# Half of the weight tiles loaded as fp32 on a hardware queue and cast on ScalarE, in a DMA-bound matmul of four windows

One core of one Trainium2 chip. The metric is the device time of one execution in microseconds (us).

## The reference

```python
B, S, D, W = 4, 4096, 4096, 64          # x: [B,S,D] fp32, w: [D,D] fp32
for b in range(B):
    o = int(offsets[b])
    results.append(x[b, o:o+W] @ w)     # [64,4096] @ [4096,4096]
return np.stack(results)                # [4,64,4096] fp32
```

The whole of w (67.1 MB) has to be read once, with 4.2 MB of x, and 4.2 MB are written. Each weight is used for only 256 rows, so the loads decide the time.

## The kernel before

Every tile of w, 128 rows (one k) by 2048 columns (one half `ng` of the output), is loaded by a DMA issued from GpSimd that casts fp32 to fp16 on its way. Only the first 128 rows of w (k = 0, both halves; called row 0 below) come as fp32 on ScalarE's queue and are cast there. The windows of x come as four casting DMAs, each to 64 partitions. They are transposed on TensorE, and then the matmuls follow the tiles of w as they land.

```python
    wh_pool = ctx.enter_context(tc.tile_pool(name="wh", bufs=24))
    ...
    nc.scalar.dma_start(out=w0_32[:], in_=w[0:P, :])
    def load(ng, ki):
        t = wh_pool.tile([P, NG], fp16, name="wh", tag="wh")
        nc.gpsimd.dma_start(out=t[:], in_=w[ki*P:(ki+1)*P, ng*NG:(ng+1)*NG])
        return t[:]
    wh[(0, 1)] = load(0, 1)
    ...                                  # for each b: o = offset of the window
        nc.gpsimd.dma_start(out=x16[g][m*WIN:(m+1)*WIN, :], in_=x[b][bass.ds(o, WIN), :])
    ...                                  # all other tiles in order of use; the
    ...                                  # very last one as four [128,512] pieces
    for ng in range(n_ng):               # 2 halves
        for ki in range(n_k - 1 if last else n_k):
            for g in range(G):           # 2 pairs of windows
                for j in range(n_sub):   # 4 PSUM banks each
                    mm(g, j, ki, wh[(ng, ki)][:, j*NT:(j+1)*NT], ki == 0, ki == n_k - 1)
        ...                              # first half: evict to stage[g]
    for g in range(G):                   # issued after all loads of w
        nc.gpsimd.dma_start(out=out[2*g:2*g+2, :, 0:NG], in_=stage[g][:])
    for j in range(n_sub):               # last k of the second half
        for g in range(G):
            mm(g, j, ki, wlast[j][:], False, True)
            ...                          # evict on ScalarE (g 0) or VectorE (g 1)
            q[g].dma_start(out=out[2*g:2*g+2, :, cs:cs+NT], in_=s[:])   # 256 KB each
```

The 2 MB of the first half's stores stand behind all loads in the casting queue. They keep the DMA engines busy while the last matmuls and evictions run.

## Time and profile before

| | before |
|---|---|
| time | 184.98 us median (184.97 to 185.01, 3 runs) |
| span of the profiled run | 183.1 us |
| last matmul of w ends, last packet of a DMA | 172.5 us, 181.3 us |

From the page of the kernel before: the bytes moved in 40 slices of the span, the chain of work that ended last, the largest group of instructions, and the issues of w tiles (size as written, median time to landing).

```profile
GB/s 179 348 221 215 207 213 215 215 214 211 213 211 214 215 213 214 214 216 214 211 214 212 213 213 214 213 215 214 215 213 212 213 214 212 213 213 205 387 403 172
...
DMA wh<-in_w_dram 90%; ACT sth L150 1%; PE bank L117 1%; ACTq L153 1%; POOLq L60 0%; POOLq L168 0%
...
L117 PE MATMUL bank<-wh,xT 128*128 128x512 f16 x488 | 113.8, 378 | 28.6 <-DMA wh<-in_w_dram 28.6
...
wh<-in_w_dram POOLq DMA_DIRECT2D x61, 512.0 KB, 19.1
```

Loads of w make up 90% of the chain, and TensorE waits for them. The slices count bytes as written. A casting load reads twice what it writes, so 213 GB/s there is 426 GB/s of reading, and the stores at the end (387 and 403 GB/s) are not a faster stage. All rates below are therefore given on the source side: casting bytes count twice, plain ones once.

The view of the DMA queues of before, for 15 to 29 us (the end of x, then w) and for 60 to 150 us; columns are packets, MB written, share of 16 engines' time. A packet is one row of a transfer; packets of 4 bytes, about one in nine, are counted with them:

```profile
q0 software_dynamic: 693, 2.97, 104.6%
```

The timeline of before (start, duration, engine, line, operation) when x arrives, and at its end:

```profile
16.17 3.57 PE L103 MATMUL bank<-identity,xrow 128*128 128x128 f16 x32 [16.17 <-DMA xrow<-in_x_dram]
...
24.35 2.07 PE L117 MATMUL bank<-w0half,xT 128*128 128x512 f16 x8
```

```profile
168.93 1.89 PE L117 MATMUL bank<-wh,xT 128*128 128x512 f16 x8 [0.57 <-DMA wh<-in_w_dram]
...
170.65 1.89 PE L117 MATMUL bank<-wl,xT 128*128 128x512 f16 x8
171.07 0.58 ACT L150 COPY sth<-bank 128x512 f32<-128x512 f32 x1 [73.36 <-PE bank L117]
...
171.69 0.34 ACTq L153 DMA_DIRECT2D out_dram<-sth  x1
```

The first matmul of w starts at 24.35 us. A tile needs 1.89 us of matmul and TensorE waits another 0.57 us for the next, so TensorE is never far behind the loads. The first store of the last group leaves 0.6 us after the first eviction (the copy of a finished sum out of PSUM) starts.

### The profile page before, as it was taken

Reading aid. Unit: us, or ns where it says so; the run is one execution under the profiler, and the core shown is the slowest. Engines: PE = TensorE matmul, PEld = TensorE weight load, DVE = VectorE, ACT = ScalarE, POOL = GpSimd, SP = SyncE. Lnnn points to the kernel's source line nnn. Section 1 sums busy time; section 2 is a strip of 40 time slices with the busy share of each in tenths; the row PEclk is TensorE's granted clock in tenths of the full one; section 3 lists DMA queues with packets and bytes.
Section 4 is the critical chain, followed back from the end, with each engine's and each line's share of the span. In section 5 each row is a group of like instructions: output and inputs, shape, how many; then the busy total and the mean of one; then the engine's idle time right before and its main releaser. Section 6 shows DMA issues by size and latency. Waiting matters only on the chain.

```text
span 183.1 us, 1380 instructions
## 1 busy us (share of the span) xinstructions
PE 126.3 (69%) x576; PEld 56.4 (31%) x576; DVE 10.5 (6%) x16; ACT 14.1 (8%) x19; POOL 38.3 (21%) x77
## 2 busy tenths in 40 slices
PE   0004799988877777887779878777777877777600
PEld 0004664433333233333324333323232333333200
DVE  0002530000000000000005000000000000000500
ACT  2081430000000000000013000000000000000310
POOL 4612221222222112222221222222122222210000
PEclk9999999999999999999999999999999999999965
DMA  6999999999999999999999999999999999999994
GB/s 179 348 221 215 207 213 215 215 214 211 213 211 214 215 213 214 214 216 214 211 214 212 213 213 214 213 215 214 215 213 212 213 214 212 213 213 205 387 403 172
DMA packets 11271, 40.97 MB, mean 224 GB/s; under 512 B 1282, under 2 KB 1794, under 8 KB 10626
## 3 DMA queue, kind: packets, MB, share of 16 engines
q0 software_dynamic: 9968, 36.70, 97.0%
q10 hardware_dynamic: 720, 3.15, 4.7%
q1 hardware_dynamic: 578, 1.05, 1.5%
q8 instruction: 4, 0.07, 0.1%
q14 instruction: 1, 0.01, 0.0%
HBM read 71.30 MB, written 4.19 MB: 412 GB/s over the span
## 4 chain that ended last, share of the span: by engine, by line
DMA 90%; issue 2%; ACT 1%; PE 1%; ACTq 1%; POOLq 0%
DMA wh<-in_w_dram 90%; ACT sth L150 1%; PE bank L117 1%; ACTq L153 1%; POOLq L60 0%; POOLq L168 0%
## 5 line engine op out<-in xcount | busy, mean ns | idle before, releaser
L117 PE MATMUL bank<-wh,xT 128*128 128x512 f16 x488 | 113.8, 378 | 28.6 <-DMA wh<-in_w_dram 28.6
L117 PEld LDWEIGHTS <-xT 128*128 128x128 f16 x512 | 49.8, 97 | 98.0 <-issue 44.1
L60 POOL DMA_DIRECT2D wh<-in_w_dram x61 | 32.4, 531 | 112.5 <-DMA wh<-in_w_dram 100.2
L103 PE MATMUL bank<-identity,xrow 128*128 128x128 f16 x64 | 7.1, 311 | 17.4 <-DMA xrow<-in_x_dram 17.4
L103 PEld LDWEIGHTS <-xrow 128*128 128x128 f16 x64 | 6.7, 147 | 17.6 <-issue 17.6
L150 ACT COPY sth<-bank 128x512 f32<-128x512 f32 x4 | 2.3, 586 | 74.6 <-PE bank L117 73.8
L137 ACT COPY stage<-bank 128x512 f32<-128x512 f32 x4 | 2.1, 600 | 70.5 <-PE bank L117 70.5
L112 DVE CAST xT<-bank 128x512 f16<-128x512 f32 x8 | 5.5, 691 | 19.3 <-PE bank L103 19.3
L152 DVE COPY sth<-bank 128x512 f32<-128x512 f32 x4 | 2.5, 683 | 72.3 <-PE bank L117 72.3
L139 DVE COPY stage<-bank 128x512 f32<-128x512 f32 x4 | 2.5, 682 | 71.7 <-PE bank L117 71.7
L114 ACT CAST xT<-bank 128x512 f16<-128x512 f32 x8 | 4.7, 586 | 6.9 <-PE bank L103 6.9
L117 PE MATMUL bank<-w0half,xT 128*128 128x512 f16 x16 | 4.3, 390 | 0.2 <-DVE stage L139 0.2
L90 POOL DMA_DIRECT2D wl<-in_w_dram x4 | 2.1, 527 | 7.5 <-DMA wh<-in_w_dram 7.5
L77 POOL DMA_DIRECT2D xrow<-in_x_dram x4 | 2.1, 520 | 2.2 <-issue 2.2
L97 ACT CAST w0half<-w0row 128x2048 f16<-128x2048 f32 x1 | 1.9, 1897 | 7.4 <-DMA w0row<-in_w_dram 7.4
L141 POOL DMA_DIRECT2D out_dram<-stage x2 | 1.1, 534 | 4.2 <-DMA wh<-in_w_dram 4.2
L98 ACT CAST w0half<-w0row 128x2048 f16<-128x2048 f32 x1 | 1.9, 1893 | 0.0
L117 PE MATMUL bank<-wl,xT 128*128 128x512 f16 x8 | 1.9, 379 | 0.0
L97 ACT ACT_TABLE_LOAD x1 | 1.3, 1283 | 1.3 <-PEq L168 1.3
masks.py:199 POOL TENSOR_SCALAR_AFFINE_SELECT identity<-identity 128x128 f16<-128x128 f16 x1 | 0.3, 287 | 0.1
masks.py:197 POOL MEMSET identity<- 128x128 f16 x1 | 0.2, 223 | 0.0
L168 POOL MEMSET const-float32-0.0<- 128x1 f32 x1 | 0.1, 98 | 0.4 <-issue 0.4
(3 smaller groups left out, 0.3 us busy)
## 6 DMA issues: line engine op xcount, KB each, us to landing
wh<-in_w_dram POOLq DMA_DIRECT2D x61, 512.0 KB, 19.1
w0row<-in_w_dram ACTq DMA_DIRECT2D x1, 2048.0 KB, 9.0
xrow<-in_x_dram POOLq DMA_DIRECT2D x4, 512.0 KB, 12.3
out_dram<-stage POOLq DMA_DIRECT2D x2, 1024.0 KB, 12.1
out_dram<-sth ACTq DMA_DIRECT2D x4, 256.0 KB, 6.5
out_dram<-sth SPq DMA_DIRECT2D x4, 256.0 KB, 6.6
wl<-in_w_dram POOLq DMA_DIRECT2D x4, 128.0 KB, 14.9
off_t<-in_offsets_dram SPq DMA_DIRECT2D x1, 0.0 KB
```

The source lines that it names most:

```text
L60: nc.gpsimd.dma_start(out=t[:], in_=w[ki * P : (ki + 1) * P, ng * NG : (ng + 1) * NG])
L77: nc.gpsimd.dma_start(out=x16[g][m * WIN : (m + 1) * WIN, :], in_=x[b][bass.ds(o, WIN), :])
L90: nc.gpsimd.dma_start(out=t[:], in_=w[ki * P : (ki + 1) * P, cs : cs + NT])
L97: nc.scalar.copy(out=w0_16[:, :NG], in_=w0_32[:, :NG])
L103: nc.tensor.matmul(out=ps[t][:, i * P : (i + 1) * P], lhsT=x16[g][:, k * P : (k + 1) * P], rhs=identity[:], start=True, stop=True,)
L112: nc.vector.tensor_copy(out=dst, in_=ps[t][:])
L114: nc.scalar.copy(out=dst, in_=ps[t][:])
L117: nc.tensor.matmul(out=ps[4 * g + j][:], lhsT=xT[g][:, ki * P : (ki + 1) * P], rhs=rhs, start=start, stop=stop,)
L137: nc.scalar.copy(out=dst, in_=ps[4 * g + j][:])
L139: nc.vector.tensor_copy(out=dst, in_=ps[4 * g + j][:])
L150: nc.scalar.copy(out=s[:], in_=ps[4 * g + j][:])
L152: nc.vector.tensor_copy(out=s[:], in_=ps[4 * g + j][:])
```

## The change

The intent is to use both ways of loading at once: even k tiles of w come as fp32 on SP's hardware queue and ScalarE, 8% busy before, casts them; odd ones stay casting loads. The last four tiles are all casting loads. The last tile is loaded whole, and the last group goes out as two 1 MB stores instead of eight of 256 KB.

```diff
-    wh_pool = ctx.enter_context(tc.tile_pool(name="wh", bufs=24))
+    wg_pool = ctx.enter_context(tc.tile_pool(name="wg", bufs=4))
+    wf_pool = ctx.enter_context(tc.tile_pool(name="wf", bufs=5))
+    wh_pool = ctx.enter_context(tc.tile_pool(name="wh", bufs=12))
 ...
     def load(ng, ki):
+        src = w[ki * P : (ki + 1) * P, ng * NG : (ng + 1) * NG]
+        if ki % 2 == 0 and (ng, ki) < (n_ng - 1, n_k - 4):
+            t = wf_pool.tile([P, NG], fp32, name="wf", tag="wf")
+            nc.sync.dma_start(out=t[:], in_=src)
+            wf[(ng, ki)] = t
+            return None
         t = wh_pool.tile([P, NG], fp16, name="wh", tag="wh")
 ...
-        for ki in range(n_k - 1 if last else n_k):
+        for ki in range(n_k):
+            if (ng, ki) in wf:
+                t = wg_pool.tile([P, NG], fp16, name="wg", tag="wg")
+                nc.scalar.copy(out=t[:], in_=wf[(ng, ki)][:])
+                wh[(ng, ki)] = t[:]
 ...                               # (the four pieces of the last tile are gone)
+            (q[g] if last else nc.gpsimd).dma_start(
+                out=out[2 * g : 2 * g + 2, :, ng * NG : (ng + 1) * NG],
+                in_=stage[ng][g][:],
+            )
```

## The prediction

> **What bounds it.** The DMA engines. The chain of waits is 90% loads of w; the slice table has DMA at 9 in 38 of 40 slices, tensor clock 9 throughout the stream. The issue table shows 61 w tiles landing in 19.1 us each with eight in flight; the chain shows eight per 19.66 us, 2.46 us a tile, so 1.05 MB read at 427 GB/s. The GB/s row says 213 because it counts the fp16 bytes written. A tile needs only 1.89 us of matmul (timeline), so TensorE waits 0.55 us per tile on the load (28.6 us in all).
>
> **Is a plain fp32 load cheaper?** Hardly. Packet records: the fp32 row 0 of w alone passed a 16 KB packet per engine every 611 ns, 429 GB/s read; casting packets pass 8 KB each 307 ns, 427 GB/s. The cast writes half the bytes but reads the same, and the time follows the bytes read. The Trainium skill, "DMA: Bandwidth & Descriptors", section "Issuing engines are not separate DMA queues", says all queues run on the same 16 engines; the trace agrees: while both queues were busy (5.5 to 8.5 us) an engine alternated one fp32 16 KB packet and one casting 8 KB packet every 923 ns, together 427 GB/s. So "both at once" adds no bandwidth: 71.3 MB read and 4.2 MB written remain, about 178 us of packets.
>
> **Removed:** 28 casting loads and their issue (0.53 us each) on GpSimd, off the chain. The last tile no longer goes in four pieces of 1 KB rows (3.1 against 2.46 us), and the last stores no longer use 2 KB rows (84 ns a packet against 309 for 8 KB): about 0.7 and 0.45 us gained.
>
> **Added:** 28 casts on ScalarE, 1.9 us each (the casts of row 0), 53 us; ScalarE was 8% busy; off the chain unless they come late. The last group's stores wait for all four evictions per half: the first leaves about 2.6 us after the first bank is done, against 0.6. ScalarE evictions no longer wait on issues (2.4 us instead of 3.7).
>
> **Moved.** Five fp32 tiles now compete with x at the start: the second half of x, landing at 20.6 us, should land near 27 to 30, first w matmul 24.4 to about 33. TensorE has slack to catch up. Afterwards odd and even tiles share the engines packet by packet, 4.9 us each; evens lead, so evens finish near 150 us, then about eight casting tiles remain, at 2.46 us. Each odd then frees two tiles (3.8 us of matmul): TensorE should lag the last landing (about 170 us) by 3 to 5 us instead of 1.4. The 2 MB of first-half stores cover 4.9 us; the engines should then stand idle 1 to 4 us before the final 2 MB (4.9 us). Worked forward with these durations, an estimate: span 183.5 to 186.5, time 1.9 more than the span as before.
>
> **Prediction:** 186.5 us, range 182.5 to 192. Chances: faster by over 2% 0.04, within 2% 0.70, slower by over 2% 0.26.
>
> **Shows it right:** read rate in the stream (bytes written weighted for the cast) still 425 to 430 GB/s; ScalarE busy near 64 us; first w matmul near 33 us; fp32 queue done near 150 us, the casting queue last; a dip of DMA between the first-half and last stores.
>
> **Makes it wrong:** the split of the engines. If the casting queue gets over about 57% the evens land last, and behind the last lie a cast and six tiles of matmul (13 us): 190 to 200. If mixing slows packets by a few per cent: 189. If mixing hides bubbles between packets and the tail stays covered: 182.

## More of the kernel before

```profile
q0 software_dynamic: 5252, 19.15, 106.0%
```

From 60 to 150 us that is 2 x 19.15 MB in 90 us, 425.6 GB/s read. This is close to what the Trainium skill's "HBM Reference" (section "Specifications (TRN2)") gives for a core that streams alone, about 425 GB/s, bounded by its 16 DMA engines.

## The result

| | before | changed |
|---|---|---|
| time, median (range, runs) | 185.0 us (184.97 to 185.09, 4) | 187.55 us (186.73 to 187.89, 4) |
| ratio, 95% interval | | 1.0131 (1.0097 to 1.0164) |
| span of the profiled run | 183.1 us | 186.0 us |
| first matmul of w | 24.35 us | 33.55 us |
| last packet of a casting load of w | 171.2 us | 174.7 us |
| last packet of a DMA | 181.3 us | 184.7 us |

A ratio here is the mean time of one kernel's fast runs over the mean of the other's of the same rounds, so it is not quite the ratio of the medians. The change made the kernel 1.3% slower, which is inside 2%. Part of the 3.4 us between the last packets comes back after them: the span ends 1.8 us after the last packet before and 1.3 us after it in the changed kernel.

The page of the changed kernel:

```profile
GB/s 183 383 306 268 263 268 290 312 286 313 321 310 321 313 320 315 319 318 314 314 314 316 315 319 311 321 313 320 314 318 315 319 320 225 213 212 214 369 308 282
...
DMA 79%; PE 12%; issue 3%; DVE 1%; POOLq 1%; POOL 1%; DVEq 0%
...
L111 PE MATMUL bank<-wh,xT 128*128 128x512 f16 x272 | 63.5, 378 | 29.3 <-DMA wh<-in_w_dram 29.3
...
L129 ACT CAST wg<-wf 128x2048 f16<-128x2048 f32 x28 | 52.5, 1903 | 56.9 <-DMA wf<-in_w_dram 53.9
...
wf<-in_w_dram SPq DMA_DIRECT2D x28, 1024.0 KB, 22.8
wh<-in_w_dram POOLq DMA_DIRECT2D x34, 512.0 KB, 39.1
```

The row of GB/s looks half as fast again as before, 316 against 213, and that is the trap of this profile: fp32 bytes written are not cast bytes written. ScalarE's 28 casts take 52.5 us and the engine waits for data in between, so they are no bottleneck. The mean of 1,903 ns agrees with an estimate from the Trainium skill, "ScalarE: Activation LUTs", section "What ACT_TABLE_LOAD costs", which gives 186 ns + 0.833 ns per element for an ACTIVATE with immediate scale and bias: 1,892 ns for 2,048 elements, if a cast counts as one.

The view of the DMA queues of the changed kernel, 15 to 29 us (x beside fp32 tiles):

```profile
q0 software_dynamic: 260, 1.72, 58.9%
q1 hardware_dynamic: 271, 1.96, 43.7%
```

And 60 to 150 us:

```profile
q1 hardware_dynamic: 2598, 18.94, 51.9%
q0 software_dynamic: 2597, 9.46, 51.8%
```

In the stream the read rate is (2 x 9.46 + 18.94) / 90 = 420.7 GB/s against 425.6, and at 15 to 29 us it is (2 x 1.72 + 1.96) / 14 = 386 GB/s. The two queues got 2,597 and 2,598 packets: an even split. This agrees with the Trainium skill, "DMA: Bandwidth & Descriptors", section "Queues, rings and completion order", which says that an engine takes the queues that have work in turn, a packet at a time. The counts show the equal turns, not how many rows an engine takes in one turn. Both shares together are 103.7% of the engines' time against 106.0% (packets overlap a little, hence over 100). A packet itself took no longer, 322 ns in the median against 324; the next one began later.

The smaller number of buffers is a rival: 12 for casting loads and 5 for fp32 ones, instead of 24. The page speaks against it. At 4.9 us a tile on each queue, landing times of 22.8 and 39.1 us mean that more than four fp32 tiles and about eight casting ones were under way at a time. And the loss is even: by the packet records the rate was 412 to 422 GB/s in every 5 us from 30 to 155 us, against 421 to 427 in before.

The timeline of the changed kernel when x arrives and at its end:

```profile
22.39 3.57 PE L97 MATMUL bank<-identity,xrow 128*128 128x128 f16 x32 [22.39 <-DMA xrow<-in_x_dram]
...
33.55 2.36 PE L111 MATMUL bank<-w0half,xT 128*128 128x512 f16 x8
```

```profile
155.80 1.90 ACT L129 CAST wg<-wf 128x2048 f16<-128x2048 f32 x1 [3.03 <-DMA wf<-in_w_dram]
...
169.24 8.80 PE L111 MATMUL bank<-wh,xT 128*128 128x512 f16 x40
176.56 2.05 ACT L138 COPY stage<-bank 128x512 f32<-128x512 f32 x4 [18.86 <-PE bank L111]
...
178.65 0.36 ACTq L142 DMA_DIRECT2D out_dram<-stage  x1
```

The last fp32 tile is cast at 155.8 us and only casting loads are left. The last store waits for its evictions and leaves at 178.65 us. The engine table of the changed kernel, in stretches of 2 us, shows the gap that this leaves (after the length come the busy times of PE, PEld, DVE, ACT and POOL, then the clock; the last two columns are DMA share and GB/s written):

```profile
178.00:180.00 2.00, 0.04 (x1) 0.00 (x0) 1.91 (x4) 0.62 (x2) 0.00 (x0) 1.00 0.47 197
180.00:182.00 2.00, 0.00 (x0) 0.00 (x0) 0.00 (x0) 0.00 (x0) 0.00 (x0) 0.82 0.96 393
```

**Where the time went.** Every kernel here moves the same 75.5 MB, counted at the source. So the time lost in a stretch can be worked out from the trace's packet records: its length minus its bytes divided by 427 GB/s, the rate of casting loads in before. The sums close: the last packet comes 3.4 us later, and the rows differ by 3.3 us. The last columns are experiments told below.

| DMA time lost, us | before | changed | a: casting only | c: x first | c2: x first, fewer fp32 | e: x in 128 rows |
|---|---|---|---|---|---|---|
| 0 to 10 us | 2.92 | 2.96 | 2.98 | 2.98 | 3.05 | 2.88 |
| 10 to 30 (x) | -0.02 | 1.48 | -0.03 | 0.03 | 0.02 | 0.15 |
| 30 to 155 (stream) | 0.21 | 1.78 | 0.21 | 1.79 | 1.67 | 1.84 |
| 155 to 170 | 0.14 | 0.01 | 0.01 | 0.13 | 0.01 | 0.01 |
| 170 to the last packet | 1.07 | 1.43 | 1.17 | 2.68 | 1.02 | 1.52 |
| of these, in the last 1 us | 0.75 | 0.09 | 0.85 | 0.09 | 0.79 | 0.10 |
| last packet at, us | 181.3 | 184.7 | 181.3 | 184.6 | 182.8 | 183.4 |

Two terms carry the loss: 1.5 us while x is loaded and 1.6 us spread over the stream. The gap at 178 to 180 us, though it catches the eye, makes the tail only 0.4 us worse than before, because the old tail lost 0.75 us in its last microsecond, where the changed kernel lost 0.09. Its small rows need not be the reason: a_cast_only, with 8 KB rows, lost 0.85 us there.

### The profile page after: what moved, and what is told of

Same layout as the page of the kernel before. It is cut to its first block, busy times and chain, and to the rows that moved or that the text cites. A ratio compares the mean times of both kernels' runs of the same rounds, so it can differ in the third digit from the quotient of the medians.

```text
span 186.0 us, 1430 instructions
## 1 busy us (share of the span) xinstructions
PE 122.0 (66%) x576; PEld 56.7 (30%) x576; DVE 10.5 (6%) x16; ACT 66.0 (36%) x47; POOL 22.0 (12%) x46
## 4 chain that ended last, share of the span: by engine, by line
DMA 79%; PE 12%; issue 3%; DVE 1%; POOLq 1%; POOL 1%; DVEq 0%
DMA wh<-in_w_dram 79%; PE bank L111 12%; DVE stage L140 1%; POOLq L75 1%; POOL xrow L82 0%; DVEq L171 0%; POOL identity masks.py:197 0%; POOLq L82 0%; POOL wh L66 0%; POOLq L66 0%; POOLq masks.py:199 0%; POOLq L160 0%
## 5 line engine op out<-in xcount | busy, mean ns | idle before, releaser
L111 PE MATMUL bank<-wh,xT 128*128 128x512 f16 x272 | 63.5, 378 | 29.3 <-DMA wh<-in_w_dram 29.3
L129 ACT CAST wg<-wf 128x2048 f16<-128x2048 f32 x28 | 52.5, 1903 | 56.9 <-DMA wf<-in_w_dram 53.9
L111 PE MATMUL bank<-wg,xT 128*128 128x512 f16 x224 | 52.9, 379 | 0.0
L66 POOL DMA_DIRECT2D wh<-in_w_dram x34 | 18.1, 535 | 132.9 <-DMA wh<-in_w_dram 113.5
L138 ACT COPY stage<-bank 128x512 f32<-128x512 f32 x8 | 4.1, 599 | 31.0 <-PE bank L111 31.0
L140 DVE COPY stage<-bank 128x512 f32<-128x512 f32 x8 | 5.0, 683 | 140.9 <-PE bank L111 140.9
## 6 DMA issues: line engine op xcount, KB each, us to landing
wf<-in_w_dram SPq DMA_DIRECT2D x28, 1024.0 KB, 22.8
wh<-in_w_dram POOLq DMA_DIRECT2D x34, 512.0 KB, 39.1
```

What stands on the lines that cost most here:

```text
L66: nc.gpsimd.dma_start(out=t[:], in_=src)
L111: nc.tensor.matmul(out=ps[4 * g + j][:], lhsT=xT[g][:, ki * P : (ki + 1) * P], rhs=rhs, start=start, stop=stop,)
L129: nc.scalar.copy(out=t[:], in_=wf[(ng, ki)][:])
L138: nc.scalar.copy(out=dst, in_=ps[4 * g + j][:])
L140: nc.vector.tensor_copy(out=dst, in_=ps[4 * g + j][:])
```

## The experiments

My theory after the result was this. The mix of fp32 and casting packets is slower than casting alone, above all beside x; the gap before the last stores adds to it. The rivals were that the new tail is the whole loss, that two queues cost by themselves, and that the slow start is mere start-up. All kernels gave correct results unless said otherwise.

### a_cast_only: the new tail without the mix

```diff
-        if ki % 2 == 0 and (ng, ki) < (n_ng - 1, n_k - 4):
+        if False:                                   # and 24 fp16 buffers again
```

> The changed kernel with every tile of w on the casting queue again (24 fp16 buffers), but the new tail kept: last tile whole, last group stored as two 1 MB DMAs. If the loss comes from mixing fp32 and casting loads (my theory: 1.4 us while x and fp32 tiles share the engines, 1.7 us in the stream), the read rate is back at 426 to 428 GB/s in every stretch of the stream, the first w matmul near 24.4 us, and the time 184 to 185.3 us, 0.985 of the changed kernel. If the loss comes from the new tail (rival), the time stays at 187 or above. A gap of the DMA before the last stores of 0.5 to 1.5 us should show in either case.

Measured: 184.07 us (183.99 to 184.21), ratio to before 0.9947 (0.9934 to 0.9960). Its queue from 60 to 150 us:

```profile
q0 software_dynamic: 5252, 19.15, 106.0%
```

The read rate is back at 425.6 GB/s in the stream, nothing is lost beside x, and the first matmul of w starts at 24.50 us. So the mix is the loss and the version without it, with the new tail, is 0.9 us faster than before. The predicted gap of 0.5 to 1.5 us was a miss: only 0.2 us were lost at 174 to 176 us.

### b_small_stores: the gap before the last stores

The changed kernel, but each bank of the last group stored (256 KB) right after its eviction.

```diff
+                if last:
+                    cs = ng * NG + j * NT
+                    q[g].dma_start(out=out[2*g:2*g+2, :, cs:cs+NT], in_=dst)
 ...                               # (no store after the loop in the last half)
```

> The changed kernel with the last group stored in eight 256 KB DMAs, each issued right after its eviction. If the dip in the DMA at 178 to 180 us is the wait for four evictions, it closes (under 0.3 us lost there instead of 1.2), the 2 KB rows cost 0.45 us, and the time falls by 0.5 to 1.0 us against the changed kernel, to about 186.8. If the stores' form does not matter, it is within 0.2 us of it.

Measured: 188.51 us (187.70 to 189.24), ratio 1.0190 (1.0166 to 1.0214). The gap closed, 0.05 us lost at 178 to 180 us, and yet the kernel was not faster. The packet records say why: the whole tail from 170 us lost 1.17 us instead of 1.43, since 0.72 us were lost in its last microsecond instead of 0.09, and the stretch of x happened to lose 1.90 us instead of 1.48. Whether the 2 KB rows cost the last microsecond is not shown: before, a_cast_only and c2_x_first_few lose 0.75 to 0.85 us there, with rows of 2 KB and of 8 KB. All of these had at most a short gap before it. Why the engines then end unevenly was not tested. The expected gain in time was wrong. A gap in the DMA is worth what the sum of its stretch says, not its own length.

### c_x_first: fp32 loads held back until x has landed

A one-element copy from x into the first fp32 buffer makes the SP queue wait for x. Nothing else changes.

```diff
 ...                                  # load() only notes fp32 tiles in `later`
+        if g == 1:                   # between the transposes of the two pairs
+            for i, (ng, ki, src) in enumerate(later):
+                t = wf_pool.tile([P, NG], fp32, name="wf", tag="wf")
+                if i == 0:
+                    nc.vector.tensor_copy(out=t[64:65, 0:1], in_=x16[1][64:65, 0:1])
+                nc.sync.dma_start(out=t[:], in_=src)
 ...
```

> The changed kernel with the fp32 queue held back until all of x has landed (a one-element copy from x into the first fp32 buffer). If fp32 packets beside x packets are what costs 1.4 us at 15 to 30 us, the read rate there is 425 to 429 GB/s instead of 383 to 390, x lands near 20.6 us and the first w matmul is near 24.4 us; the stream after it stays at 421. The last packet then comes 1.2 to 1.6 us sooner and the time is near 186.1 if the tail is no worse; evens will finish later, near 160 us. Rival: the rate is low there because the program starts and queues fill; then holding back the fp32 queue moves the slow stretch to later and gains nothing.

Measured: 187.59 us (187.41 to 188.18), ratio 1.0147 (1.0131 to 1.0162). The start did what the theory says: 428.9 GB/s at 15 to 20 us, x landed by 20.4 us, first matmul of w at 24.21 us, 0.03 us lost instead of 1.48. The rival of a mere start-up is out. But no time was gained. The timeline of this kernel's end says where it went:

```profile
165.51 1.90 ACT L135 CAST wg<-wf 128x2048 f16<-128x2048 f32 x1 [3.00 <-DMA wf<-in_w_dram]
167.46 1.89 PE L117 MATMUL bank<-wg,xT 128*128 128x512 f16 x8 [1.29 <-ACT wg L135]
169.18 8.80 PE L117 MATMUL bank<-wh,xT 128*128 128x512 f16 x40
176.50 2.05 ACT L144 COPY stage<-bank 128x512 f32<-128x512 f32 x4 [9.10 <-PE bank L117]
...
178.59 0.35 ACTq L148 DMA_DIRECT2D out_dram<-stage  x1
```

The fp32 queue started some 18 us later, and its last tile was there at 165.5 us, ten us later than in the changed kernel. Behind it stood a cast of 1.9 us and six tiles of matmul, 10.5 us. The matmuls ended at 178.0 us (169.18 + 8.80), as in the changed kernel (169.24 + 8.80), though the last casting packet had come at 173.1 us instead of 174.7. The engines ran dry waiting for the last stores: the tail lost 2.68 us. What the start gained, a new wait at the end took.

### c2_x_first_few: the same, with fewer fp32 tiles

To test that reading, the fp32 loads stop at k = 18 of the second half, and the last 12 tiles are casting loads.

```diff
-        if ki % 2 == 0 and (ng, ki) < (n_ng - 1, n_k - 4):
+        if ki % 2 == 0 and (ng, ki) < (n_ng - 1, n_k - 12):
```

> The fp32 queue held back until x has landed, and fp32 only up to the 18th tile of the second half, so that the last 12 tiles are casting loads. With x first alone, the start was fast again (428 GB/s) and no time was gained: my reading is that the last fp32 tile then landed at 165.4, and its cast and six tiles of matmul (12 us) ended TensorE at 177.4, with 2.5 us of idle DMA before the last stores. If so, here TensorE ends 2 to 2.5 us after the last casting load, the idle DMA falls to 0.2 to 0.7 us and the time to 185.0 to 185.8. If the start gains nothing for another reason, it stays at 187 or above.

Measured: 185.93 us (185.85 to 186.12), ratio 1.0053 (1.0040 to 1.0066), a little above the range that I gave. Its end:

```profile
173.36 1.89 PE L117 MATMUL bank<-wh,xT 128*128 128x512 f16 x8 [0.65 <-DMA wh<-in_w_dram]
173.77 2.05 ACT L144 COPY stage<-bank 128x512 f32<-128x512 f32 x4 [25.88 <-PE bank L117]
```

TensorE follows the last load (last packet 172.98 us) again, and the tail loses 1.02 us. So both were real: the 1.5 us of the start, and the wait that hid them. What is left against a_cast_only, 185.93 against 184.07 us, is the stream: 1.67 against 0.21 us lost there.

### e_x_128_rows: why fp32 is slow beside x

The result is wrong: x is loaded as two DMAs of 128 (wrong) rows instead of four of 64. Bytes and packets of x are the same, 16 KB read and 8 KB written.

```diff
-        nc.gpsimd.dma_start(out=x16[g][m*WIN:(m+1)*WIN, :], in_=x[b][bass.ds(o, WIN), :])
 ...                               # (the loop over four windows becomes one over two pairs)
+        nc.gpsimd.dma_start(out=x16[g][:], in_=x[2 * g][0:P, :])
```

> Wrong result on purpose: the changed kernel with x loaded as two DMAs of 128 rows each (wrong rows), the same bytes and the same 16 KB packets, instead of four of 64 rows. If fp32 packets are slow beside x because each x DMA writes only half of the partitions (my theory), the read rate at 15 to 28 us is 418 to 427 GB/s. If long casting packets beside fp32 packets are the cause (rival), it stays at 375 to 392.

Measured: 186.66 us (186.44 to 187.00), ratio 1.0096 (1.0081 to 1.0111). Its queues at 15 to 29 us:

```profile
q0 software_dynamic: 287, 1.90, 65.0%
q1 hardware_dynamic: 291, 2.12, 37.4%
```

That is (2 x 1.90 + 2.12) / 14 = 423 GB/s instead of 386, and 0.15 us lost at 10 to 30 us instead of 1.48. So it is not the packet length of x. What the edit changed is the number of rows of each x load; with it went half as many DMAs and fixed source rows, which were not tested alone. In the changed kernel x's own packets keep their 624 ns there and the fp32 packets stretch from 322 ns to a median of 388 (14 to 28 us); with 128 rows they keep 322. The Trainium skill, "SBUF — State Buffer", section "Door 1: The DMA port swizzle", gives a likely cause: partitions 0 to 63 reach only 8 of the 16 DMA ports of SBUF, with an asymptote of about 218 GB/s written. Alone, x writes 214 GB/s (428.9 / 2), just under that, because the cast halves it. An estimate with that page's figure: alternating x and fp32 packets at 427 GB/s read would write 142 GB/s of each, and 142 + 71 = 213 GB/s to the crowded half, which leaves no room for unevenness. That the form of x's loads matters is shown; that it is the 64 rows, and that the ports are the reason, is argued.

### d_fp32_only, f_fp32_two_queues, g_fp32_two_tiles: why the stream is slower

```diff
-        if ki % 2 == 0 and (ng, ki) < (n_ng - 1, n_k - 4):
+        if (ng, ki) != (0, 1):       # d: all others fp32 on SP, 9 fp32 buffers
                                      # f: even k on SP's queue, odd k on ACT's
                                      # g: k > 1, two tiles in one 2 MB DMA on SP
 ...                                  # (buffers to match)
```

> All tiles of w but one as fp32 on the SP queue, cast on ScalarE (61 casts, 116 us). This asks whether 421 GB/s in the stream is the price of fp32 packets or of two queues side by side. If two queues side by side: 426 to 429 GB/s from 40 to 95 us here. If fp32 DMAs of 8 KB rows are slower themselves: about 415 (twice the loss of the mix). The time itself is not the test, since the last tile has to be cast and the first half's stores go out in the middle: 185 to 192 us.

> All of w as fp32, even tiles on the SP queue and odd ones on the ACT queue. One fp32 queue alone read 421 to 422 GB/s, casting alone 426.5, both together 421 instead of the 424 that their mean would give. If two queues side by side cost by themselves, 416 to 419 GB/s here between 40 and 95 us; if not, 421 to 422. The time is not the test (about 195).

> All of w but a few tiles as fp32 on the SP queue, two tiles to a DMA (2 MB, the same 8 KB packets, half as many DMAs). If the 1.2% that plain fp32 loads lose to casting ones is paid per DMA, 423.5 to 425 GB/s between 40 and 95 us; if it is paid per packet, 421 to 422. The time is not the test (about 195).

Measured: d 195.32 us (194.31 to 196.15), ratio 1.0562 (1.0528 to 1.0596); f 198.55 us and g 198.78 us (about 195 expected), one run each, state unknown. The view of the DMA queues of d, 60 to 150 us (its q0 are the first half's plain stores):

```profile
q1 hardware_dynamic: 4921, 35.87, 95.7%
q0 software_dynamic: 288, 2.10, 5.5%
```

Plain fp32 loads alone move (35.87 + 2.10) / 90 = 421.9 GB/s. That is neither of the values that I had named (426 to 429, or about 415): the mix is as slow as plain loads alone, not half way. Two hardware queues, f, moved 420.6 to 422.7 GB/s from 60 to 100 us, so a second queue does not cost by itself; from 40 to 60 us that run did not keep the engines busy (387 GB/s), so the window that I had named was partly a miss. Two tiles to a DMA, g, gave 421.3 to 421.7 GB/s from 60 to 100 us, so half as many DMAs change nothing. The 0.9% thus belongs to plain loads of 8 KB rows on hardware queues. A plain load on GpSimd's queue, or one of longer rows, was not run as a stream, so queue, cast and row length are not told apart. A hint is that the plain 16 KB packets of row 0, alone for a moment in before, passed at 611 ns each, 429 GB/s. Why casting loads slow down beside them to the same 421 stays open. The time of d was above its range for a known reason: the last tile landed, was cast and multiplied before anything could be stored, and the engines stood idle from 179 to 186 us.

### after_again, b2_half_stores, c3_x_first_half_stores, a2_cast_half_stores: the stores once more

Stores of 512 KB after every two evictions, put into the changed kernel (b2), into c_x_first (c3) and into a_cast_only (a2), with the changed kernel itself run again.

```diff
+                if last and j % 2 == 1:
+                    lo, hi = (j - 1) * NT, (j + 1) * NT
+                    q[g].dma_start(out=out[2*g:2*g+2, :, ng*NG+lo:ng*NG+hi],
+                                   in_=stage[ng][g][:, lo:hi])
 ...                               # (no store after the loop in the last half)
```

> The changed kernel itself again, so that the next runs have it in the same rounds and on the same chip: ratio 1.013 to before, and its scatter (186.7 to 187.9 before) seen again. Profile: 374 to 392 GB/s read in the stretch where x and fp32 tiles share the engines, 421 in the stream, a gap near 178 to 180 us.

> The eight small stores closed the gap and did not make it faster, against my expectation. Here the last group goes out in four 512 KB stores with 4 KB rows, each after two evictions. If the gap costs time and only the 2 KB rows and a slower start ate the gain in that run: gap under 0.6 us, time 0.4 to 0.8 us below the changed kernel of these rounds. If the gap is worth nothing because something else ends the program: within 0.2 us of it.

> x first (the quiet start) with the last group in four 512 KB stores. The store tests on the changed kernel were lost in its scatter; here the start is steady, and the gap before the last stores was 2.5 us. If the wait for all four evictions is worth what the gap shows, the first stores begin 0.8 to 1 us sooner and the time is 186.6 to 187.0 against 187.6 (ratio 1.009 to 1.011 against 1.0147). If not, 1.013 or above.

> Only casting loads and the last tile whole, as in the run that was 0.53% faster than before, with the last group now in four 512 KB stores. There the idle DMA before the last stores was 0.23 us only, so 0.0 to 0.3 us are to be had: 183.8 to 184.1 us, ratio 0.993 to 0.995. The fastest version if anything.

| | time, us | ratio to before |
|---|---|---|
| after_again | 188.81 (186.77 to 190.65, 6 runs) | 1.0205 (1.0169 to 1.0241), unclear |
| b2_half_stores | 187.71 (187.55 to 188.85) | 1.0144 (1.0130 to 1.0159) |
| c3_x_first_half_stores | 187.71 (187.44 to 187.95) | 1.0140 (1.0125 to 1.0156) |
| a2_cast_half_stores | 184.16 (184.11 to 184.20) | 0.9952 (0.9938 to 0.9965) |

Three of the six runs of after_again count as slow, being over 1.5% above its fastest; the three others are 186.77, 187.79 and 188.03 us, as before. The ratio in the table fits the mean of all six; the three fast runs alone give 1.014. Their clock says nothing against the slow ones being the same scatter: 0.970 to 0.980 in these, 0.965 to 0.991 in the fast ones. So 1.3% may understate what the change costs in the mean. Against that scatter b2 decides nothing. Where the scatter is small, earlier stores gained nothing: c3 is level with c_x_first (187.71 and 187.59), against my expectation of 0.6 to 1.0 us, and a2 with a_cast_only (184.16 and 184.07), where 0.0 to 0.3 us were expected. In the profile of c3 the tail still lost 2.49 us against 2.68. Its TensorE ended at 178.65 us, 0.7 us later than in c_x_first, because the last fp32 tile came later, and that ate what the earlier stores gave in this profile. What waits at the end is the matmuls, not the form of the stores.

The scatter has a pattern. Kernels with fp32 packets beside 64-row x spread by 1.2 us or more (the changed kernel, b, b2, d), and in four profiles of the changed kernel, b and b2 the stretch of x lost 1.13 to 2.27 us. In the profiles of d, f and g, where fp32 tiles also came beside x, it lost 2.01, 1.82 and 3.39 us. Kernels without that overlap spread by 0.1 to 0.8 us (a, a2, c, c2, c3, e). That the overlap causes the scatter is likely but was not tested by itself.

## Why the prediction was right

The measured 187.55 us lies in the range of 182.5 to 192, 1 us above the point, and "within 2%" was given 0.70. The structure was right. That the point is only 1 us off is partly luck, since the last casting packet came 4.7 us later than forecast.

- **Right: no added bandwidth.** Both queues run on the same engines and take turns (2,598 and 2,597 packets). The statement of the Trainium skill, "DMA: Bandwidth & Descriptors", section "Issuing engines are not separate DMA queues", that spreading DMAs over issuing engines saves only issue time, held.
- **Right: the moves.** x landing "near 27 to 30" us was 29.1, the first w matmul "about 33" was 33.55, ScalarE "near 64 us" busy was 66.0. The fp32 queue finished near 155.8 us (predicted 150, so 6 us late), the casting queue last. TensorE ended 3.3 us after the last casting packet (178.0 and 174.7 us; predicted 3 to 5 us).
- **Right in size, not in place: the tail's gains.** "About 0.7 and 0.45 us" were to be saved on the DMA engines, and a_cast_only is 0.9 us faster than before. But from 155 us to the last packet before lost 1.21 us and a_cast_only 1.18, and the last packet of both came at 181.3 us. In these two profiles the spans differ by 0.5 us, all of it after the last packet (1.8 us against 1.2); the rest of the 0.9 us is in no profile. So these profiles do not show the two savings, and why the end after the last packet is shorter stays open.
- **Mis-sized: the packets.** "71.3 MB read and 4.2 MB written remain, about 178 us of packets" took the mixed packets at the rate of casting ones, and the read rate in the stream was to be "still 425 to 430 GB/s". It was 420.7 in the stream (1.6 us) and 386 beside x (1.5 us). The first part I had named only as a risk ("if mixing slows packets by a few per cent: 189"); that x's 64 rows matter I had not seen. The last casting packet came at 174.7 us instead of about 170. In before it came at 171.2 us: the two terms are 3.1 of the 3.5 us between, and the forecast saving on the last tile does not show.
- **Over-rated: the idle engines.** "Idle 1 to 4 us before the final 2 MB" did happen, about 1.2 us, but against the tail before it cost only 0.4 us. The idle time came out at the low end of its range and the packets took longer than forecast, so the two partly cancelled.
- **The named danger did not happen here, but did in c_x_first.** "Behind the last lie a cast and six tiles of matmul" became true as soon as the fp32 queue started later.

The fastest version of all is a_cast_only, 184.07 us, 0.5% faster than before: only the part of the change that touches the tail is worth keeping.

## What to carry to other kernels

When the DMA engines are the limit, ask how many source bytes per engine and second each form of load moves; here a second queue and a second form only shared that, and lowered it a little (420.7 GB/s against 425.6 in the stream, 386 beside x). Count casting loads on the read side, since a profile that counts written bytes will show a gain that is none. When a start-up loss is removed and the time does not move, look for the work that stands behind the last load of each stream: its order of arrival may have changed.

## What the Trainium skill lacked or had wrong

- "DMA: Bandwidth & Descriptors" has no rate for casting loads. Here a casting load runs at the rate of its source bytes: 425.6 GB/s read for 8 KB rows, 428.9 for 16 KB rows of x.
- The same page calls the hardware queues generally faster. For the two forms used here it was the other way round: plain fp32 loads of 8 KB rows on SP's queue moved 421.9 GB/s, 0.9% less than casting loads on GpSimd's, with one tile or two to a DMA; a mix of both also moved only 420.7. The same plain load on both queues was not compared, so the page's statement itself was not tested. No page has these rates.
- "SBUF — State Buffer" gives the half-port rate for a 64-partition DMA alone. It does not say that such a DMA, itself at full rate (428.9 GB/s read, 214 written), can slow another queue's 128-partition loads beside it: 386 GB/s in all against 423 when x had 128 rows, and by a different amount from profile to profile (1.13 to 2.27 us lost in four).
